# The end of a feed-forward sweep: gated residual on seven sums and one accumulation for the last two down steps, in all three sweeps

## The chip, the core and the metric

The kernel runs on one core of a Trainium2 chip. The core has five engines with their own instruction streams: TensorE (PE, matrix products), VectorE (DVE), ScalarE (ACT), GpSimd (POOL) and SyncE (SP, which here issues all transfers between the DRAM and the on-chip memory). Matrix products are written to PSUM, of which this part of the kernel uses eight banks of 512 columns. The metric is the time of one execution on the device in microseconds (us).

## The reference

One layer of a diffusion backbone on 2048 latent tokens and 128 context tokens of width 1024. A first half (two kinds of linear recurrence between an input and an output projection) gives the residual stream `x2`. The second half, which the change touches, is

```
h  = rms_norm(x, norm2) * (1 + sc2) + sh2
ff = (silu(h @ w_gate) * (h @ w_up)) @ w_down      # 1024 -> 2816 -> 1024
x  = x + g2 * ff
y  = rms_norm(x, norm_f)
```

`g2` is a row of 1024 gates, one row for all latent tokens and another for the context tokens. All is float32.

## The kernel before

The tokens are 17 tiles of 128 rows. The feed-forward part runs in three sweeps over tiles: sweep 0 has 5 (the context tile `NL` first, then four of latent tokens), sweeps 1 and 2 have 6 latent tiles each. In each sweep the hidden width is walked in 11 steps `fp` (0 to 10) of 256 columns. A step computes the gate product and the up product of its columns for all tiles of the sweep (two calls of `unit`), multiplies them (L1476) and multiplies the result by 256 rows of `w_down` (a down step), which is added to the sweep's output `acc`, one tile of 128x1024 for each tile of tokens.

Each float32 factor is split into a high and a low part (`split`: ACT rounds, DVE or POOL subtracts), and a product is three matmuls. `unit` multiplies by blocks with seven products in place of eight (`z`, L1209): 12 matmuls a product, 14 products in a step. In sweep 0 the weight parts for this are made (loads `wr`, sums on POOL, splits) and also stored to DRAM (`wpd`); sweeps 1 and 2 load them from there (`wp`, 512 KB a part, four buffers). In sweeps 1 and 2 the down steps 0 to 8 also work by seven sums (`down_seven`, y of L1367), which `combine` puts together in step 9. Step 9 and 10 of every sweep, and all steps of sweep 0, are plain (`down`, y of L1406: groups of six matmuls for one step, one tile of tokens and one half `n` of the 1024 columns), added to `acc` from PSUM by DVE (L1410).

Groups of a down step are not run at once: they are put in the list `pending`, and `unit` takes some from it after each of its products (`tick`). The groups of the last two steps (`rest`) run behind step 10.

The end of a sweep differs. In the last sweep step 10 loads the gate `g2` and puts one `residual` for each tile in `pending`: DVE multiplies `acc` by the gate (L1252), POOL adds `x2` from DRAM (L1253). The last two down steps are then one group of twelve matmuls for each tile and half; DVE multiplies it by the gate out of PSUM (L1413, tile `yg`), POOL adds it to `acc` (L1415, DVE for the last tile), and `finish` normalises the tile (squares `jk` on ACT, small instructions on DVE, a last one at L1262) and stores it. The four blocks of `w_down` of step 10 (`wds10`) are put in `wp` buffers. In sweeps 0 and 1 the last two steps are two groups of six with two adds on DVE, and residual and finish of each tile (`close`) are put in `pending` in step 0 of the next sweep.

Behind step 10 of sweeps 0 and 1 the token parts of the next sweep (`stored_parts`, loads `hr`, splits into `x1` to `x7`) and the first weight parts (`uw`) are also prepared.

Two sets of buffers are shared by much of this: `raw6`, four tiles of 128x1024 (`wr`, `wdr` for the rows of `w_down`, `hr`, `x2`, the gate, `norm_f`), and `wp`. There are three PSUM banks for `y` and five for `z`. A list scheduler sets the order of instructions on each engine when the program is built, by program order and its own estimate of times; on the chip each engine keeps that order.

Of the kernel before, what the change touches and what calls it, by code (L numbers as in the profile page):

```python
# [33 lines left out]
def hybrid_step(ctx: ExitStack, tc, x, vecs, ada1, ada2, bada, win, wgt, alog, dtb, sa, sb, wout, wg, wu, wd, normf,  # L34
# [1008 lines left out]
    with ExitStack() as s6:  # L1043
# [232 lines left out]
        def wd_part(a, tile=None):  # L1276
            t = halves_of(tile() if tile else fl.tile([P, 2, 512], F32R, tag="wd", name="wd", bufs=5))
            split(a, *t)
            return t

        def wd_blocks(fp, tile=None):

            out = {}
            rs = wd_raw(fp)
            for n in range(2):
                for j in range(2):
                    out[n, j] = wd_part(rs[j][:, 512 * n:512 * n + 512], tile)
            return out
# [98 lines left out]
        def down(ts_, steps, N, first=False, end=False):  # L1387

            n2 = len(ts_) // 2
            if end:  # L1390
                nf = load_nf()

            def group(ti, n):
# [17 lines left out]
                else:  # L1411
                    yg = fe.tile([P, 512], F32, tag="st", name="yg", bufs=2)
                    nc.vector.tensor_tensor(out=yg, in0=py, in1=g2[0][:, cs], op=ALU.mult)  # L1413
                    e = nc.vector if ti == len(ts_) - 1 else nc.gpsimd
                    e.tensor_tensor(out=acc[c][:, cs], in0=yg, in1=acc[c][:, cs], op=ALU.add)  # L1415
                if n and end:
                    finish(c, acc[c], nf)

            idx = range(len(ts_))
            return [lambda i=i, n=n: group(i, n) for i, n in  # L1420
                    ([(i, n) for i in idx for n in range(2)] if end else [(i, n) for n in range(2) for i in idx])]

# [10 lines left out]
        for sw, ts_ in enumerate(sweeps):  # L1433
# [9 lines left out]
            for fp in range(NP):  # L1443
                if fp == 0 and sw:

                    nf = load_nf()
                    g2[0] = load_g2()

                    def close(c):
                        residual(c)  # L1450
                        finish(c, acc[c], nf)

                    pending.extend([lambda c=c: close(c) for c in sweeps[sw - 1]])
                if fp == NP - 1:
                    wds9 = wd_blocks(NP - 2)
                    if last:
                        g2[0] = load_g2()
                        pending.extend([lambda c=c: residual(c) for c in ts_])
# [31 lines left out]
            wds10 = wd_blocks(NP - 1, (lambda: wp_tile().rearrange("p a k f -> p a (k f)")) if last else None)  # L1490
            if last:
                rest = down(ts_, [(last_hid, wds9), (hid, wds10)], N, end=True)
            else:
                rest = down(ts_, [(last_hid, wds9)], N) + down(ts_, [(hid, wds10)], N)
# [65 lines left out]
```

## Time and profile before

| what | value |
|---|---|
| median of 3 runs | 3359.61 us (3348.92 to 3360.17) |
| the profiled execution | 3358.57 us, span of the trace 3356.9 us |
| PE busy | 3121.5 us, 93% of the span |
| DVE, ACT, POOL busy | 2089.0, 1519.0, 1254.8 us |
| the feed-forward sweeps | some 1860 to 3357 us of the span |

Times in rows are us from the start of the span. A row of the windows view gives the stretch, its length, then for each engine the time it was busy and (x) its instructions, the granted clock of TensorE as a share of full speed, the share of time that the 16 transfer engines were busy, and GB/s. A row of the timeline gives start, length, engine, line, instruction, out<-in, shape and, in brackets, the idle time before it and what ended it. Matmuls are pipelined: the length of one reaches into the next, so the pitch is read from the starts.

### The profile page before, as it was taken

How to read it: one execution, taken by the hardware profiler on the slowest of the kernel's cores; microseconds unless marked ns; L12 is line 12 of the kernel's file. 1: busy time of each engine (PE TensorE's matmuls, PEld its weight loads, DVE VectorE, ACT ScalarE, POOL GpSimd, SP SyncE). 2: the span in 40 equal slices, each digit the busy share in tenths (PEclk: the TensorE clock that was granted, in tenths of full speed). 3: DMA queues.
4: the chain of work that ended last, by engine and by line, in shares of the span. 5: the costliest groups of instructions: out<-in, count | busy, mean ns of one | idle time of the engine just before them, and what ended most of it. 6: DMA issues, size and time to landing. Idle time of an engine off the chain costs nothing. (4 is left out here: it accounts for less than half of the span.)

```text
span 3356.9 us, 51604 instructions
## 1 busy us (share of the span) xinstructions
PE 3121.5 (93%) x18550; PEld 2792.2 (83%) x18550; DVE 2089.0 (62%) x4016; ACT 1519.0 (45%) x3233; POOL 1254.8 (37%) x1228
## 2 busy tenths in 40 slices
PE   7899989999999799998897999999999999899998
PEld 4687779999998677877786888888899998799997
DVE  4667744474553764564666777778565677565667
ACT  6455435374464544663764555454422223422222
POOL 1100001021121337413566544554545553544446
PEclk8999999999999988999998999999999999999999
DMA  5235410111114667877784877898656766655564
GB/s 221 72 109 145 116 55 29 53 44 36 53 39 138 172 179 230 265 249 253 240 263 152 304 287 286 298 325 314 223 192 212 240 211 230 228 193 194 184 201 155
DMA packets 331009, 620.12 MB, mean 185 GB/s; under 512 B 77818, under 2 KB 177954, under 8 KB 324354
## 3 DMA queue, kind: packets, MB, share of 16 engines
q1 hardware_dynamic: 330754, 616.83, 56.0%
q8 instruction: 147, 2.41, 0.3%
q14 instruction: 108, 0.88, 0.1%
HBM read 435.22 MB, written 181.51 MB: 184 GB/s over the span
## 5 line engine op out<-in xcount | busy, mean ns | idle before, releaser
L257 PE MATMUL pj<-hh,wh 128*128 128x384 f32 (+2 forms) x1480 | 546.0, 369 | 12.9 <-DVE q L464 6.6
L257 PE MATMUL pj<-hl,wh 128*128 128x384 f32 (+2 forms) x1480 | 545.2, 368 | 0.3 <-POOL hl L231 0.3
L257 PE MATMUL pj<-hh,wl 128*128 128x384 f32 (+2 forms) x1480 | 545.3, 369 | 0.0
L257 PEld LDWEIGHTS pj<-hh,wh 128*128 128x128 f32 (+1 forms) x1480 | 280.4, 189 | 45.5 <-DVE q L464 6.8
L257 PEld LDWEIGHTS pj<-hl,wh 128*128 128x128 f32 (+1 forms) x1480 | 280.1, 189 | 29.9 <-issue 3.1
L257 PEld LDWEIGHTS pj<-hh,wl 128*128 128x128 f32 (+1 forms) x1480 | 280.1, 189 | 28.7 <-issue 3.3
L1476 POOL TENSOR_TENSOR u<-u,g 128x384 f32<-128x384 f32 (+1 forms) x132 | 136.3, 1033 | 292.7 <-DVE u L1217 242.8
L494 POOL TENSOR_SCALAR th<-th,nlbh,lbh 128x384 f32<-128x384 f32 (+1 forms) x40 | 60.5, 1513 | 405.8 <-ACT G L492 401.8
L1371 DVE TENSOR_TENSOR acc<-y,acc 128x512 f32<-128x512 f32 x192 | 131.7, 688 | 64.9 <-PE y L1367 58.0
L1209 PE MATMUL z<-x1h,wp 128*128 128x384 f32 (+1 forms) x528 | 142.8, 334 | 17.6 <-ACT wp L1067 14.2
L1067 ACT ACTIVATE wd<-wdr 128x512 fp32r<-128x512 f32 x146 | 90.0, 627 | 149.4 <-PE y L1367 95.4
L1367 PE MATMUL y<-wd,hid0h 128*128 128x512 f32 x432 | 136.4, 399 | 18.7 <-ACT hid0h L1067 10.0
L1464 ACT ACTIVATE g<-g 128x384 f32<-128x384 f32 (+1 forms) x132 | 66.7, 505 | 191.0 <-DVE g L1217 190.1
L1067 ACT ACTIVATE hid0h<-u 128x384 fp32r<-128x384 f32 (+3 forms) x113 | 53.3, 481 | 217.2 <-POOL u L1476 181.2
L1209 PE MATMUL z<-x6h,wp 128*128 128x384 f32 (+1 forms) x528 | 142.7, 333 | 7.2 <-ACT wp L1067 4.6
L246 DVE TENSOR_TENSOR wl<-raw,wh 128x512 fp32r<-128x512 f32 (+1 forms) x74 | 51.7, 698 | 153.6 <-ACT wh L245 153.5
L1371 DVE TENSOR_TENSOR sum<-y,sum 128x512 f32<-128x512 f32 x144 | 99.3, 690 | 75.8 <-PE y L1367 73.3
L1209 PE MATMUL z<-x4h,wp 128*128 128x384 f32 (+1 forms) x528 | 144.5, 331 | 1.3 <-DMA wp<-wpd 1.3
L1209 PE MATMUL z<-x7h,wp 128*128 128x384 f32 (+1 forms) x528 | 144.3, 332 | 1.0 <-DMA wp<-wpd 1.0
L1068 DVE TENSOR_TENSOR wd<-wdr,wd 128x512 fp32r<-128x512 f32 x146 | 111.9, 775 | 51.5 <-ACT wd L1067 50.6
L1209 PE MATMUL z<-x3h,wp 128*128 128x384 f32 (+1 forms) x528 | 142.6, 328 | 0.0
L1209 PE MATMUL z<-x2h,wp 128*128 128x384 f32 (+1 forms) x528 | 140.5, 328 | 1.4 <-DMA wp<-wpd 1.4
(414 smaller groups left out, 8850.6 us busy)
## 6 DMA issues: line engine op xcount, KB each, us to landing
wp<-wpd SPq DMA_DIRECT2D x308, 512.0 KB
wpd<-wp SPq DMA_DIRECT2D x154, 512.0 KB
ld<-qkvd SPq DMA_DIRECT2D x34, 1024.0 KB
wdr<-in_wd_dram SPq DMA_DIRECT2D x66, 512.0 KB
raw<-in_win_dram SPq DMA_DIRECT2D x72, 256.0 KB
e<-grd SPq DMA_DIRECT2D x68, 256.0 KB
at<-in_ada_dram SPq DMA_DIRECT2D x64, 256.0 KB
wr<-in_wg_dram SPq DMA_DIRECT2D x22, 512.0 KB
```

Of the source, the lines that this page charges most:

```text
L246: nc.vector.tensor_tensor(out=wl[:, ks], in0=raw, in1=wh[:, ks], op=ALU.subtract)
L257: nc.tensor.matmul(out=out, lhsT=a[:, k], rhs=b[:, k], start=t == 0, stop=t == 3 * KD - 1)
L494: nc.gpsimd.tensor_scalar(out=th, in0=th, scalar1=nlbh[:, col:col + 1], scalar2=lbh[:, col:col + 1], op0=ALU.mult, op1=ALU.add)
L1067: nc.scalar.activation(out=wh, in_=raw, func=AF.Copy)
L1068: (e or nc.vector).tensor_tensor(out=wl, in0=raw, in1=wh, op=ALU.subtract)
L1209: nc.tensor.matmul(out=z, lhsT=w_[:, k], rhs=x_[:, k, :N], start=t == 0, stop=t == 3 * HK - 1)
L1367: nc.tensor.matmul(out=py, lhsT=u_[:, j * P:j * P + P], rhs=v_, start=t == 0, stop=t == 2)
L1371: nc.vector.tensor_tensor(out=sums[i, j], in0=py, in1=sums[i, j], op=ALU.add)
L1464: nc.scalar.activation(out=g, in_=g, func=AF.Silu)
L1476: nc.gpsimd.tensor_tensor(out=us[i], in0=us[i], in1=gs[i], op=ALU.mult)
```

## The change

In all three sweeps the gate is loaded and the residual runs in step 10 (on what the first nine steps have summed), and the last two down steps are one group of twelve matmuls whose result is multiplied by the gate and added. In sweeps 0 and 1 `finish` stays in `pending` of step 0 of the next sweep; the last sweep keeps its finish behind each tile (`lastone`). The context tile has its own gate, which `gate2` loads once in its residual and once in its down groups; its two groups run first, one behind the other. Three of the four blocks `wds10` are put in `wp` buffers in sweeps 0 and 1, the fourth in a `wd` buffer (in the last sweep all four, as before).

```diff
-        def wd_part(a, tile=None):
-            t = halves_of(tile() if tile else fl.tile([P, 2, 512], F32R, tag="wd", name="wd", bufs=5))
+        def wd_part(a, lent=False):
+            t = halves_of(wp_tile().rearrange("p a k f -> p a (k f)") if lent
+                          else fl.tile([P, 2, 512], F32R, tag="wd", name="wd", bufs=5))
...
-                    out[n, j] = wd_part(rs[j][:, 512 * n:512 * n + 512], tile)
+                    out[n, j] = wd_part(rs[j][:, 512 * n:512 * n + 512], 2 * n + j < lent)
...
-        def down(ts_, steps, N, first=False, end=False):
+        def down(ts_, steps, N, first=False, end=False, lastone=False):
...
-            if end:
+            if lastone:
                 nf = load_nf()
+            gm = {}
...
                 else:
+                    if c not in gm:
+                        gm[c] = gate2(c)
                     yg = fe.tile([P, 512], F32, tag="st", name="yg", bufs=2)
-                    nc.vector.tensor_tensor(out=yg, in0=py, in1=g2[0][:, cs], op=ALU.mult)
-                    e = nc.vector if ti == len(ts_) - 1 else nc.gpsimd
+                    nc.vector.tensor_tensor(out=yg, in0=py, in1=gm[c][:, cs], op=ALU.mult)
+                    e = nc.vector if lastone and ti == len(ts_) - 1 else nc.gpsimd
                     e.tensor_tensor(out=acc[c][:, cs], in0=yg, in1=acc[c][:, cs], op=ALU.add)
-                if n and end:
+                if n and lastone:
                     finish(c, acc[c], nf)
...
+            own = [(i, n) for i in idx for n in range(2) if lastone or end and ts_[i] == NL]
             return [lambda i=i, n=n: group(i, n) for i, n in
-                    ([(i, n) for i in idx for n in range(2)] if end else [(i, n) for n in range(2) for i in idx])]
+                    own + [(i, n) for n in range(2) for i in idx if (i, n) not in own]]
...
                     nf = load_nf()
-                    g2[0] = load_g2()
-
-                    def close(c):
-                        residual(c)
-                        finish(c, acc[c], nf)
-
-                    pending.extend([lambda c=c: close(c) for c in sweeps[sw - 1]])
+                    pending.extend([lambda c=c: finish(c, acc[c], nf) for c in sweeps[sw - 1]])
                 if fp == NP - 1:
                     wds9 = wd_blocks(NP - 2)
-                    if last:
-                        g2[0] = load_g2()
-                        pending.extend([lambda c=c: residual(c) for c in ts_])
+                    g2[0] = load_g2()
+                    pending.extend([lambda c=c: residual(c) for c in ts_])
...
-            wds10 = wd_blocks(NP - 1, (lambda: wp_tile().rearrange("p a k f -> p a (k f)")) if last else None)
-            if last:
-                rest = down(ts_, [(last_hid, wds9), (hid, wds10)], N, end=True)
-            else:
-                rest = down(ts_, [(last_hid, wds9)], N) + down(ts_, [(hid, wds10)], N)
+            wds10 = wd_blocks(NP - 1, 3 + last)
+            rest = down(ts_, [(last_hid, wds9), (hid, wds10)], N, end=True, lastone=last)
+            if not last:
                 fresh_parts()
```

## Rows read from the trace of the kernel before

**Rows 1.** Windows view, stretches of the feed-forward part.

```profile
2252.00:2266.00 14.00, 14.00 (x87) 13.21 (x86) 11.19 (x20) 6.13 (x12) 5.15 (x5) 1.00 1.00 372
2266.00:2280.00 14.00, 14.00 (x97) 14.00 (x96) 9.52 (x13) 7.08 (x16) 14.00 (x12) 1.00 0.81 298
2280.00:2293.00 13.00, 12.89 (x85) 12.36 (x84) 9.28 (x16) 5.26 (x10) 6.35 (x8) 1.00 1.01 374
2293.00:2325.00 32.00, 31.75 (x144) 26.19 (x143) 30.58 (x47) 16.22 (x30) 4.99 (x6) 1.00 0.87 309
2325.00:2376.00 51.00, 36.99 (x180) 33.32 (x179) 38.77 (x64) 22.78 (x52) 29.64 (x20) 0.90 0.83 281
2797.00:2851.00 54.00, 52.50 (x253) 45.33 (x251) 42.39 (x62) 20.29 (x40) 12.70 (x8) 1.00 0.63 206
2851.00:2895.00 44.00, 31.02 (x132) 27.45 (x132) 33.47 (x59) 22.40 (x47) 31.59 (x24) 0.85 0.77 262
2925.00:3250.00 325.00, 325.00 (x1703) 304.35 (x1702) 197.50 (x310) 81.34 (x150) 153.60 (x142) 1.00 0.59 193
3260.00:3317.00 57.00, 53.05 (x277) 49.91 (x276) 43.53 (x47) 9.40 (x18) 49.61 (x29) 0.97 0.67 227
```

**Rows 2.** Waits of PE, 2330 to 2400: us in total, times, longest.

```profile
PE y L1367 <- ACT wd L1067: 7.1, 1, 7.1
PE z L1209 <- DMA wp<-wpd: 2.5, 3, 1.4
PE y L1367 <- POOL hid0l L1068: 2.0, 1, 2.0
```

**Rows 3.** Timeline of ACT at the first seam.

```profile
2351.80 0.63 ACT L747 ACTIVATE jk<-acc 128x512 f32<-128x512 f32 x1 [1.77 <-POOL acc L1253]
...
2353.04 0.61 ACT L1067 ACTIVATE wd<-wdr 128x512 fp32r<-128x512 f32 x1
```

**Rows 4.** Waits of PE, 2845 to 2920.

```profile
PE y L1367 <- ACT hid0h L1067: 8.6, 2, 6.7
PE y L1367 <- ACT acc L1369: 2.9, 1, 2.9
```

**Rows 5.** Timeline of PE, two products behind the wait at 2353.71.

```profile
2355.15 0.52 PE L1209 MATMUL z<-x4h,wp 128*128 128x384 f32 x1
...
2358.67 0.52 PE L1209 MATMUL z<-x4h,wp 128*128 128x384 f32 x1
...
2361.61 0.34 PE L1209 MATMUL z<-x5h,wp 128*128 128x384 f32 x1
...
2363.73 0.34 PE L1209 MATMUL z<-x3h,wp 128*128 128x384 f32 x1
```

**Rows 6.** Instructions by source line: count, ns min/median/max, first and last start.

```profile
L1410 DVE TENSOR_TENSOR acc<-y,acc x124: 671/678/692, 1929.8 to 2849.8; 128x512 f32<-128x512 f32 x124
...
L1252 DVE TENSOR_TENSOR acc<-acc,g x17: 1199/1435/3396, 2320.3 to 3290.7; 128x1024 f32<-128x1024 f32 x17
...
L1253 POOL TENSOR_TENSOR acc<-acc,x x17: 2337/2392/3354, 2327.5 to 3302.9; 128x1024 f32<-128x1024 f32 x17
...
L1415 POOL TENSOR_TENSOR acc<-yg,acc x10: 1283/1292/1312, 3319.3 to 3343.1; 128x512 f32<-128x512 f32 x10
```

**Rows 7.** Waits of PE at the end of the last sweep, 3285 to 3357.

```profile
PE z L1209 <- DVE g L1217: 2.4, 1, 2.4
```

**Rows 8.** Timeline of POOL at the end of sweep 0.

```profile
2262.91 1.29 POOL L1071 TENSOR_TENSOR s<-wr 128x512 f32<-128x512 f32 x1 [3.94 <-DMA wr<-in_wg_dram]
...
2298.22 1.47 POOL L1068 TENSOR_TENSOR hid0l<-u,hid0h 128x256 fp32r<-128x256 f32 x2
```

**Rows 9.** Timeline of PE, last product of sweep 0 and first groups behind it.

```profile
2292.80 0.31 PE L1209 MATMUL z<-x3h,wp 128*128 128x320 f32 x1
2292.94 0.63 PE L1406 MATMUL y<-wd,hid0h 128*128 128x512 f32 x2
...
2294.33 0.62 PE L1406 MATMUL y<-wd,hid0h 128*128 128x512 f32 x2
```

More of the change, by code (lines that the diff above doesn't have):

```diff
@@ L1274, in wd_raw, with wd_blocks @@
             return rs
-        def wd_part(a, tile=None):
-            t = halves_of(tile() if tile else fl.tile([P, 2, 512], F32R, tag="wd", name="wd", bufs=5))
+        def wd_part(a, lent=False):
+            t = halves_of(wp_tile().rearrange("p a k f -> p a (k f)") if lent
+                          else fl.tile([P, 2, 512], F32R, tag="wd", name="wd", bufs=5))
             split(a, *t)
             return t
-        def wd_blocks(fp, tile=None):
+        def wd_blocks(fp, lent=0):
             out = {}
```

## The prediction, made before the changed kernel ran

> **What bounds the kernel now.** I read the page first, for the engines' shares, then cut the feed-forward part into stretches by the windows view, then asked the waits of TensorE (PE) in the stretches where it was not full, and last the timeline of single engines there. The page's shares say that PE bounds the whole, so a change to the other engines is worth only the PE time that it frees or takes. The windows [rows 1] show where there is any: in the steady part of the third sweep PE is busy 325.00 of 325 us, but at the seam of sweeps 0 and 1 (2325 to 2376) it is busy 36.99 of 51 us, so 14.0 us idle, and at the seam of sweeps 1 and 2 (2851 to 2895) 31.02 of 44 us, so 13.0 us. The down steps just ahead of that second seam (2797 to 2851) lose another 1.5 us. These 28.5 us are all that the edit can free directly.
>
> What ends the idle time there? At the first seam one wait of 7.1 us for ScalarE's (ACT) split of a `wd` tile, 2.0 us for a POOL split of `hid0l`, and 2.5 us for `wp` loads [rows 2]. The long one is a queue: on ACT the square of the norm (`jk`) stood ahead of the `wd` split and itself waited 1.77 us for POOL's residual add; the split came right behind it [rows 3]. At the second seam ACT again is what PE waits for, 8.6 us for `hid0h` and 2.9 us for the first `acc` of the new sweep, whose buffer the old sweep's finish still held [rows 4]. So residual and finish of the old sweep, run in step 0 of the next, are what stalls PE at both seams.
>
> PE also pays in clock. Behind the 7.1 us wait a product of 12 matmuls takes 2355.15 to 2359.19 = 4.04 us; the next product's 12 run from 2361.61 to the start of the one behind it at 2363.73, 2.12 us [rows 5]. That is the lower of the clock's two levels, and costs 1.9 us per seam stall. At the second seam two waits (6.7 and 2.9 us) come before such a product and the mean granted clock is 0.85 [rows 1, 4]; I take 3 us there.
>
> Recoverable in all: 14.0 + 1.9 + 13.0 + 3 + 1.5 = 33.4 us.
>
> **The change, part by part.** *Matmuls.* The same products in the same number, 12 in a group in place of twice 6. Worth 0 for PE.
>
> *Evacuation.* The 124 adds of L1410 [rows 6] include 2 x 5 x 2 = 20 of the last two steps of sweep 0 and 24 of sweep 1; they become 10 and 12 multiplications by the gate of the same size on VectorE (DVE), and as many adds on POOL at 1.29 us [rows 6]. At their 0.68 us sweep 0 saves 10 x 0.68 = 6.8 us of DVE in a stretch where DVE is busy 30.58 of 32 us (2293 to 2325), and POOL, busy 4.99 us there, takes on 12.9 [rows 1]. PE idles only 0.25 us there, so this gives next to nothing itself; it is room.
>
> *The residual* leaves step 0 of the next sweep: 5 and 6 gate multiplications (1.2 to 3.4 us each on DVE) and POOL adds of 2.39 us [rows 6], with their `x2_d` loads on SP. Only `finish` stays. At the seam this takes 12 and 14 us of POOL work and 7 to 9 us of DVE work away, and lets the first `wd` rows be loaded without waiting behind the residual's tiles in `raw6`. The finish itself can start tile by tile during the last down groups, and PE has the next 14 products (some 30 us at 2.12 us each) before it needs the first `wd`. So I let the ACT and POOL waits go. What is late next is the `wp` load: `wds10` now sits in three of four `wp` tiles until its groups are done, so where four weight parts of the next sweep lay ready at the seam, one does. A product lasts 2.12 us, which gives a following load about three products' time. The waits on these loads were 2.5 and about 1 us; I leave 4 us at each seam (bounds 1 and 8). Gain at the seams: 33.4 - 8 = 25.4 us.
>
> *Where the residual goes:* step 10 of sweeps 0 and 1. The last sweep already has it there and is the model for sweep 1: from 3260 to 3317 PE is busy 53.05 of 57 us [rows 1], 3.95 us idle, of which 2.4 us is a wait for a DVE evacuation of `z` standing behind residual work [rows 7]. Sweep 1 pays 4 us (bounds 1 and 7).
>
> For sweep 0 the trace has no model, and it is the crowded one: it also splits and stores the weights. In step 10 the DMA share is 1.00, 0.81 and 1.01 in three stretches from 2252 to 2293, and POOL is busy 14.00 of 14 us in the middle one [rows 1]. Into it go five residual loads and two gate loads (the context tile loads its own gate twice, in the residual and in its down groups), 7 x 0.52 MB = 3.7 MB, 9.9 us at the 372 GB/s of the first stretch; 5 POOL adds, 12 us; and the gate tile keeps one of four `raw6` slots to the sweep's end. Queued behind the loads on SP are the weights of step 10, and POOL already stands 3.94 us for such a load [rows 8]. From below the cost is 0: the holes of the 0.81 stretch (2.7 us) and later loads of `hr` absorb the bytes, and the adds run from 2300 on, where POOL is free, as late as the first new add into `acc`. From above 9.9 + 12 = 22 us, everything exposed. I take 8, nearer to the lower end, because what must be on time for PE is weights alone, and these need POOL for only part of their seven parts.
>
> *The new chain needs step 10's `hid` and `wds10` at its seventh matmul.* Before, 10 groups of 1.4 us (2292.94 to 2294.33 for the first [rows 9]) of step 9 stood ahead. In sweep 0 the last product starts its last matmul at 2292.80 and the last `hid` split ends at 2298.22 + 1.47 = 2299.69 [rows 8, 9], 6.9 us. The groups of the first half of the tokens come first, three of 2.8 us in sweep 1 and at least three in sweep 0, and need only the early two of the four `us`, so 8.4 us cover 6.9. Cost 0; without that cover 5 us per sweep. `wds10` in lent `wp` tiles is within the 8 us and 4 us taken.
>
> **Sum.** -25.4 + 4 + 8 = -13.4 us on the profiled execution's 3358.57 us: 3345.2. The median of the runs is 1.0 us above that execution, so 3346.
>
> A rule speaks against the edit: the Trainium skill (SBUF — State Buffer, Who interferes with whom) has a DVE instruction with two SBUF inputs contend with a GpSimd one that reads SBUF. The `x` splits of the next sweep are such instructions; the gate multiplication out of PSUM is not. The trace agrees as far as L1252, two SBUF inputs, ranges from 1199 to 3396 ns [rows 6]; rival D is what it would make.
>
> **The rivals.** *A, all of sweep 0's cost is hidden* and each seam keeps 2 us: -33.4 + 4 + 4 = -25, 3335 us. For it: POOL is nearly idle from 2300 to 2325 and the DMA has holes. Against it: shares of 1.00.
>
> *B, the weights starve (slower).* Place: `raw6` in step 10 of sweep 0. Two weight pairs are wanted there together; the gate tile leaves three slots, and residual tiles, earlier in the program, take the third and then those of the first pair. Each of the step's two units then waits for a pair that is loaded only when the pair before is freed: 2 x 0.52 MB at 372 GB/s 2.8 us, two POOL sums 2.6 us, a split 1.3 us, in all 6.7 us, twice, with 12 us of residual adds ahead of the sums on POOL: 25 us; with the 4 of sweep 1 that is 29 against 25.4, so 3363. It decides from 21 us on in sweep 0; with late `hid` and low clock behind every stall it reaches 41 us there, 45 in all, and 3379. For it: POOL waits for just these loads already [rows 8]. Against: PE is full in the two stretches up to 2280 [rows 1] with that load as late as it is.
>
> *C, the stall is replaced.* `finish` with its ACT chain stays in the same step and holds `acc` and ACT as before, half of each seam's loss stays (17 us): -17 + 12 = -5, 3355 us. For it: the square `jk` now waits for a POOL add that comes only behind the last down group. Against it: 30 us of products lie between.
>
> *D, DVE bounds the last groups of sweep 0.* If every POOL add held up a split for its whole length, DVE's 30.6 us become 30.6 - 6.8 + 12.9 = 36.7 us where PE needs some 32: 4.7 us more at the first seam, -8.7, 3351 us. Against: in the stretch with POOL at 14.00 of 14, DVE still did 9.52 us of work [rows 1].
>
> **How the numbers follow.** Half a per cent, 16.8 us, is about what a measurement of this kernel tells from no change. Chances: the forecast 0.38 (3336 to 3354), A 0.24, B 0.18, C 0.12, D 0.08. Faster by over 0.5% means below 3342.8: nearly all of A and a third of the forecast, 0.35. Slower by over 0.5% is above 3376.4: two thirds of B, 0.12. Same: 0.53. The range reaches from below A (3328, the whole 33.4 us less 2) to the middle of B's reach (3370), leaving out some 0.07 below and 0.12 above.
>
> **What would show it.** Right: at both seams PE's idle time falls from 14.0 and 13.0 us to 4 or less, with the ACT waits for `wd` and `hid0h` gone from its list; `wp` loads head it. Sweep 1's step 10 shows a wait of 2 to 3 us for DVE on `z`; sweep 0's step 10 shows waits for `wp` splits of 8 us in sum. Wrong: stalls of over 10 us in step 10 of sweep 0 (B), or ACT waits that stay at the seams (C), or evacuations that hold PE between 2293 and 2325 (D).

## The result and the profile after

The changed kernel takes 3385.86 us (median of 4 runs, 3380.64 to 3390.26), the kernel before 3355.07 us beside it; the ratio is 1.0092, 95% interval [1.0066, 1.0118]. It is slower by 0.9%, outside the range of the prediction. The profiled execution has a span of 3388.4 us, against 3356.9. PE's busy time is 6.0 us longer, 3127.5 us against 3121.5; the other 25.5 us of the loss are idle time.

To place it I cut every trace at the last matmul of each sweep's last product (`z<-x3h`, as 2292.80 in [rows 9]). Sweep 0, from its first product to there, went from 444.4 to 465.9 us (+21.5); the second stretch, to the same point of sweep 1, from 502.3 to 520.4 (+18.1); the third from 521.0 to 510.2 (-10.8). With 2.5 us of a later first product and 0.3 us in the tail that is 31.6 us, for the 31.5 between the spans.

These cuts lie at the same product, not at the same amount of PE's work. Counted in the traces, the changed kernel has run 12 more matmuls of down steps ahead of the first cut (558 against 546) and 16 more ahead of the second (1248 against 1232), because the first halves of its long groups start early. At some 0.23 us each (six from 2292.94 to 2294.33 in [rows 9]) 2.8 us of sweep 0's 21.5 are work done early, 0.9 us of the second stretch's 18.1, and the third stretch owes 3.7 of its 10.8 us to the same.

The windows view after, to be read against [rows 1] (PE is the first pair behind the length, the clock the third number from the right):

```profile
2252.00:2317.00 65.00, 50.05 (x299) 46.70 (x298) 39.11 (x57) 20.18 (x41) 35.42 (x28) 0.89 0.81 281
2317.00:2342.00 25.00, 10.28 (x32) 6.95 (x30) 18.15 (x27) 15.82 (x30) 6.20 (x7) 0.66 0.87 301
2342.00:2400.00 58.00, 52.18 (x239) 46.58 (x240) 31.36 (x67) 22.88 (x46) 25.98 (x20) 0.91 0.66 220
...
2830.00:2880.00 50.00, 43.69 (x195) 37.03 (x194) 36.98 (x49) 21.92 (x42) 24.92 (x18) 0.93 0.56 194
2880.00:2930.00 50.00, 44.96 (x241) 42.11 (x240) 28.02 (x69) 27.66 (x57) 27.00 (x22) 1.00 0.86 295
```

Step 10 of sweep 0, where PE had been all but full, now idles 15.0 us; the first seam idles 14.7 + 5.8 = 20.5 us where it had idled 14.0; at the second seam 5.0 us are left of 13.0, but 6.3 us are new just ahead of it (2830 to 2880). In step 10 and in the first part of the seam (2252 to 2342) the DMA share is 0.81 to 0.87 and POOL and DVE have idle time: no engine is full there.

The waits of PE after, first 2250 to 2400, then 2770 to 2960, stand against [rows 2, 4]:

```profile
PE z L1209 <- ACT wp L1067: 13.3, 2, 12.7
...
PE z L1209 <- ACT x1h L1067: 11.1, 1, 11.1
PE z L1209 <- DMA wp<-wpd: 3.4, 2, 3.2
PE y L1368 <- ACT hid0h L1067: 2.4, 1, 2.4
PE y L1409 <- DVE yg L1418: 1.8, 1, 1.8
...
PE z L1209 <- DVE u L1217: 2.2, 1, 2.2
PE z L1209 <- DMA wp<-wpd: 1.7, 3, 1.1
...
PE y L1409 <- DVE yg L1418: 6.3, 1, 6.3
PE y L1368 <- ACT hid0h L1067: 2.3, 1, 2.3
```

The 7.1 us for `wd` and the 8.6 us for `hid0h` are gone from the seams, as meant. Four waits of the new ending itself have come: 12.7, 11.1, 1.8 and 6.3 us. The first names ACT, but ACT only waits too; SP's timeline shows for what:

```profile
2257.59 0.32 SPq L1242 DMA_DIRECT2D g<-modd  x1
...
2269.27 0.36 SPq L1251 DMA_DIRECT2D x<-x2d  x1
...
2282.89 0.41 SPq L1242 DMA_DIRECT2D g<-modd  x1
...
2286.99 8.15 SPq L1251 DMA_DIRECT2D x<-x2d  x4
2297.12 0.33 SPq L1093 DMA_DIRECT2D wr<-in_wu_dram  x1
2299.42 0.33 SPq L1094 DMA_DIRECT2D wr<-in_wu_dram  x1
...
2337.20 0.32 SPq L1242 DMA_DIRECT2D g<-modd  x1
```

The second weights of step 10 (`wr` of `wu`) are loaded 19.7 us ahead of the sweep's last matmul (2316.78). In the trace before they were loaded 32.6 us ahead of it:

```profile
2260.22 0.88 SPq L1093 DMA_DIRECT2D wr<-in_wu_dram  x1
2261.19 0.44 SPq L1094 DMA_DIRECT2D wr<-in_wu_dram  x1
```

Ahead of them in the program stand the residual's tiles, all in `raw6`: the latent gate, five `x2` rows, and the context tile's own gate, which is issued only at 2282.89. SP keeps its order as the engines do, and its waits from 2255 to 2305 show two reasons for the delay. The stores of weight parts (L1103) between the loads wait for DVE's splits, and loads wait for tiles that POOL's adds still use (L1251 `x2`, L1093 and L1094 the weights):

```profile
SPq L1103 <- DVE wp L1068: 27.3, 12, 7.5
SPq L1251 <- POOL acc L1253: 4.4, 2, 2.4
SPq L1093 <- POOL acc L1253: 1.9, 1, 1.9
SPq L1094 <- POOL acc L1253: 1.9, 1, 1.9
```

PE's first matmul with the late weights is the first of these rows:

```profile
2302.14 0.64 PE L1209 MATMUL z<-x1h,wp 128*128 128x320 f32 x1 [12.72 <-ACT wp L1067]
...
2335.90 0.69 PE L1209 MATMUL z<-x1h,wp 128*128 128x384 f32 x1 [11.08 <-ACT x1h L1067]
...
2341.98 0.74 PE L1409 MATMUL y<-wd,hid0h 128*128 128x512 f32 x2 [1.79 <-DVE yg L1418]
```

The second row is the next sweep's first product, which waits for ACT's split of a late `hr` row. It stands on PE's queue behind the third of the ten long groups and ahead of the other seven, for the first three (two of them the context tile's) keep all three `y` banks until the context gate, loaded at 2337.20 behind the `hr` rows, lets DVE evacuate them:

```profile
2341.24 1.29 DVE L1418 TENSOR_TENSOR yg<-y,g 128x512 f32<-128x512 f32 x2 [1.17 <-DMA g<-modd]
```

### The profile page after: what moved, and what is told of

It reads as the page before. It is cut to its first block, busy times and chain, and to the rows that moved or that the text cites. A ratio compares the mean times of both kernels' runs of the same rounds, so it can differ in the third digit from the quotient of the medians.

```text
span 3388.4 us, 51627 instructions
## 1 busy us (share of the span) xinstructions
PE 3127.5 (92%) x18550; PEld 2795.2 (82%) x18550; DVE 2068.0 (61%) x3994; ACT 1521.1 (45%) x3235; POOL 1288.9 (38%) x1250
## 4 chain that ended last, share of the span: by engine, by line
PE 38%; DMA 7%; POOL 5%; DVE 5%; ACT 4%; issue 3%; SPq 1%; POOLq 0%; DVEq 0%; ACTq 0%
PE z L1209 18%; PE y L1368 8%; PE py L847 3%; PE y L1409 3%; DMA wdr<-in_wd_dram 1%; PE pS L938 1%; POOL u L1475 1%; DMA wp<-wpd 1%; PE po L947 1%; ACT L126 1%; PE pa L954 1%; ACT jk L747 1%; DVE wp L1068 1%; POOL acc L1253 1%; PE pj L257 1%
## 5 line engine op out<-in xcount | busy, mean ns | idle before, releaser
L494 POOL TENSOR_SCALAR th<-th,nlbh,lbh 128x384 f32<-128x384 f32 (+1 forms) x40 | 60.6, 1515 | 405.3 <-ACT G L492 401.4
L1209 PE MATMUL z<-x6h,wp 128*128 128x384 f32 (+1 forms) x528 | 143.5, 335 | 13.4 <-ACT wp L1067 5.5
L1217 DVE TENSOR_TENSOR u<-z,u 128x384 f32<-128x384 f32 (+1 forms) x165 | 84.9, 531 | 92.3 <-PE z L1209 91.3
L1209 PE MATMUL z<-x5h,wp 128*128 128x384 f32 (+1 forms) x528 | 139.9, 328 | 0.3 <-DMA wp<-wpd 0.3
```

Of the source, the lines that this page charges most:

```text
L494: nc.gpsimd.tensor_scalar(out=th, in0=th, scalar1=nlbh[:, col:col + 1], scalar2=lbh[:, col:col + 1], op0=ALU.mult, op1=ALU.add)
L1209: nc.tensor.matmul(out=z, lhsT=w_[:, k], rhs=x_[:, k, :N], start=t == 0, stop=t == 3 * HK - 1)
L1217: nc.vector.tensor_tensor(out=out, in0=z, in1=b, op=ALU.add)
```

## The experiments

The theories at the start: **S**, the four slots of `raw6`; **T**, throughput (bytes, POOL's and DVE's work of the residual in step 10); **Q**, the order of the program and of the queues; **L**, the long groups of twelve. Stretches are from one profiled execution each. Sweep 0 in the old form reads 443.6 to 448.2 us in six traces, so less than 5 us of difference there says nothing by itself. Most of that scatter lies in its first nine steps, which read 382.6 to 388.0 us over all runs. The last two, where the residual's work went, can be read closer: the column "steps 9, 10" runs from the first matmul of step 9's first product to the last one of the sweep's last product, 336 matmuls of products in each run, with the number of down-step matmuls between them in brackets. The old form reads 60.6 to 62.4 us there. Of each edit the telling lines are shown; `...` stands for lines left out.

| run | ratio, 95% interval | sweep 0 | steps 9, 10 | second | third |
|---|---|---|---|---|---|
| before | 1 | 444.4 | 61.0 (48) | 502.3 | 521.0 |
| after | 1.0092 [1.0066, 1.0118] | 465.9 | 81.2 (60) | 520.4 | 510.2 |
| e1 sweep 0 as before | 1.0008 [0.9995, 1.0021] | 446.3 | 60.8 (48) | 510.0 | 509.3 |
| e4 joined groups alone | 0.9998 [0.9982, 1.0013] | 445.7 | 60.6 (48) | 505.5 | 514.6 |
| e3 weights first | 1.0098 [1.0081, 1.0115] | 449.9 | 67.3 (60) | 535.3 | 510.6 |
| e2 gates apart | 1.0076 [1.0058, 1.0093] | 461.2 | 75.0 (60) | 515.1 | 516.2 |
| e6 no x2 add | 1.0098 [1.0082, 1.0114] | 464.6 | 77.4 (60) | 522.0 | 509.8 |
| e7 context gate kept | 1.0062 [1.0050, 1.0075] | 466.5 | 80.6 (60) | 508.3 | 510.1 |
| e5 gates and x2 aside | 1.0054 [1.0041, 1.0067] | 458.0 | 73.5 (60) | 511.9 | 514.8 |
| e11 e5 without x2 | 1.0041 [1.0026, 1.0055] | 451.9 | 67.4 (55) | 509.3 | 514.9 |
| e13 e5 without residual | 1.0030 [1.0016, 1.0043] | 449.6 | 62.9 (56) | 511.3 | 515.3 |
| e9 e2 and blocks apart | 1.0053 [1.0038, 1.0069] | 462.4 | 74.4 (60) | 515.7 | 513.1 |
| e12 e11 and blocks aside | 1.0023 [1.0008, 1.0038] | 450.8 | 65.6 (56) | 507.0 | 515.6 |
| e8 e1, sweep 1 aside | 1.0009 [0.9993, 1.0025] | 448.2 | 62.3 (48) | 506.2 | 512.1 |
| e10 e8 and blocks aside | 1.0009 [0.9998, 1.0020] | 448.0 | 62.4 (56) | 506.6 | 510.6 |
| e14 x2 left at the finish | 1.0018 [1.0004, 1.0033] | 453.9 | 68.2 (56) | 512.5 | 508.0 |
| e15 the same, sweep 1 alone | 0.9986 [0.9975, 0.9997] | 443.6 | 60.8 (48) | 509.2 | 504.1 |

**e1, sweep 0 ends in the old way, sweep 1 in the new.**

```diff
-                    g2[0] = load_g2()
-                    pending.extend([lambda c=c: residual(c) for c in ts_])
+                    if sw:
+                        g2[0] = load_g2()
+                        pending.extend([lambda c=c: residual(c) for c in ts_])
...
```

> Sweep 0 ends as in the kernel before (residual and finish in step 0 of sweep 1, two groups of six), sweep 1 ends in the new way. Clock of the sweeps, from the trace: first product of sweep 0 to its last 444.4 us before and 465.9 us changed, last of sweep 0 to last of sweep 1 502.3 and 520.4, last of sweep 1 to last of sweep 2 521.0 and 510.2. Theory S (slots: the gate and the residual's tiles in raw6 make the weights and token parts of sweep 0 late): the loss belongs to sweep 0, so 444, 506 (4 more for the residual in step 10 of sweep 1) and 510: some 7 us faster than before, ratio 0.998. Rival T (throughput: bytes, POOL and DVE work of the residual are too much in step 10 of sweep 0): the same here. Rival L (the long groups themselves cost, in any sweep): the third stretch stays at 516 or more, no faster than before.

3355.46 us against 3352.5. The whole loss is gone with sweep 0's part. Sweep 1's part gains 11.7 us in the third stretch and gives back 7.7 in the second; 3.7 us of both are 16 matmuls that run ahead of the cut between them. PE waits 2.2 us for `u` ahead of that cut and 5.8 us for `yg` behind it (to 2815.53, the cut is at 2805.90).

**e4, the kernel before with the two last down steps joined, and three blocks in `wp`; the residual stays where it was.**

```diff
...
-                rest = down(ts_, [(last_hid, wds9)], N) + down(ts_, [(hid, wds10)], N)
+                rest = down(ts_, [(last_hid, wds9), (hid, wds10)], N)
```

> The kernel before, with the last two down steps of sweeps 0 and 1 in one group of twelve and one DVE add, and three of the last blocks in wp tiles; no gate, residual and finish stay in step 0 of the next sweep. S, T, Q: within 5 us of before (3350 to 3360), seams as before. L: slower by 6 to 15 us, from waits of the long groups for the last blocks and for DVE ahead of the seam.

3350.84 us: no change that can be told. L falls. The waits for `wp` loads at the seams are 5.2 and 4.8 us in sum, so the lent blocks are felt, but they take the place of others.

**e3, sweep 0's residual put into `pending` behind the second weights.**

```diff
-                    pending.extend([lambda c=c: residual(c) for c in ts_])
+                    if sw:
+                        pending.extend([lambda c=c: residual(c) for c in ts_])
...
                 uw = weight_parts(1, fp, sw)
+                if fp == NP - 1 and not sw:
+                    pending.extend([lambda c=c: residual(c) for c in ts_])
```

> The changed kernel, with the residuals of sweep 0 put in the list only behind the loads of the second weights of step 10 (program order alone; slots, bytes and work as in the changed kernel). Theory Q (queue: the residual's loads stand ahead of the weights in program order, slots would do): the wait of 12.7 us goes, first stretch below 453, second no longer than 520, total 3365 to 3375. S: what the weights win the residual and the token parts lose, since the same tiles share the same slots: first stretch 453 to 458, second 525 to 532, total 3378 to 3390. T: as S.

3383.44 us. The 12.7 us wait is gone and comes back one user later, on the rows of `w_down`:

```profile
PE y L1409 <- ACT wp L1067: 17.6, 1, 17.6
...
PE z L1209 <- ACT x1h L1067: 11.7, 1, 11.7
```

Q as the cause falls: another order moves the wait and removes none of it. S and T both allow this.

**e2, the gates in idle tiles of the seven sums.**

```diff
-            gm = raw_tile("g2")
-            dma(out=gm, in_=mod_d[c2:c2 + 1, 3 * D:4 * D].broadcast_to([P, D]))
+            for n in range(2):
+                t = f"sum{(1, 5)[c2]}{n}"
+                gm.append(fl.tile([P, 512], F32, tag=t, name=t))
+                dma(out=gm[n], in_=mod_d[c2:c2 + 1, 3 * D + 512 * n:3 * D + 512 * n + 512].broadcast_to([P, 512]))
```

> The changed kernel, with the gates in tiles of the seven sums (idle in sweep 0, free after they are put together in sweeps 1 and 2) in place of two raw6 tiles; same bytes, same work, the residual's multiplication in two halves. S: the wait of 12.7 us for the second weights of step 10 falls below 6, the context gate comes early and the 11.1 and 1.8 us waits behind it fall below 5 together; first stretch 452 to 458 in place of 465.9, second 505 to 512 in place of 520.4; 3352 to 3366 us in all. T: all waits stay within 3 us, 3380 to 3390. L: no change in the third stretch.

3376.36 us, by the ratios some 5 us less than the changed kernel, with intervals that overlap. The waits of 12.7, 11.1 and 1.8 us are gone; in their place stand 4.8 us for DVE and 3.0 us for ACT on `wp`, 8.9 and 7.6 us for `wp` loads at the seams and 6.9 us for `u` in sweep 1. The slots taken by the gates are a part of the loss only.

**e6, POOL's add of `x2` in sweep 0 left out.**

```diff
-            nc.gpsimd.tensor_tensor(out=y, in0=y, in1=x2, op=ALU.add)
+            if c not in sweeps[0]:
+                nc.gpsimd.tensor_tensor(out=y, in0=y, in1=x2, op=ALU.add)
```

> The changed kernel with POOL's add of x2 in the residual of sweep 0 left out (five adds of 2.4 us; the x2 rows are still loaded into raw6, the gate multiplication stays): a tile is free as soon as its row has landed. Theory S, with the slots held because POOL's adds come late: the 12.7 us wait falls to 4 us or less and the ratio comes down from 1.009 to 1.003 to 1.006 (the context gate's 11.1 us stay). Theory T with the bytes as the bound: the wait stays above 9 us, ratio 1.007 or more. Together with the run that moves the tiles: if both take the wait away it is slots held by POOL; if only this one does it is POOL's work itself.

3388.53 us, ratio 1.0098: nothing gained, though POOL does 12 us less. Waits of 9.0 us for `wp` and 14.3 us for `x1h` stay. Steps 9 and 10 are 3.8 us shorter, but the wait for `x1h` is 3.2 us longer. So S in the form "slots held by POOL's adds" is refuted as the main cause, and so is T with POOL as the engine. The result is as T with the bytes foretold it; the tiles still pass through `raw6` ahead of the weights, though, so bytes and slots aren't told apart here. The next run but one does that.

**e7, the context tile's gate loaded once and kept.**

```diff
-            return load_g2(1)
+            if not cg:
+                for n in range(2):
+                    cg.append(fl.tile([P, 512], F32, tag=f"sum5{n}", name=f"cg{n}"))
+                    dma(out=cg[n], in_=mod_d[1:2, 3 * D + 512 * n:3 * D + 512 * n + 512].broadcast_to([P, 512]))
+            return cg
```

> The changed kernel with the context tile's gate loaded once, in the residual, and kept in two idle sum tiles until the context tile's groups; all else stays. If the late second load of that gate behind the hr rows is a cause of its own: the 11.1 us wait on x1h and the 1.8 us on yg at the first seam fall to 3 us or less in sum, and the time falls by 8 to 13 us, ratio 1.005 to 1.007. If it is only a shadow of the late weights (everything behind the 12.7 us wait is late anyway): less than 4 us of gain, ratio 1.008 or more, and waits for x1h or wp stay at that place.

3376.14 us. The second stretch falls by 12.1 us, with the waits for `x1h` and `yg` at the first seam, and sweep 0 is as in the changed kernel (466.5). So the late gate is a cause of its own, about 10 us by the ratios and 12 by the stretch. The interval lies apart from that of e6, measured beside it, though not from the wide one of the changed kernel itself. On PE's queue the groups now run on where the next sweep's product had stood.

**e5, gates and `x2` rows of sweeps 0 and 1 in idle sum tiles.**

```diff
+                    t = "sum" + ("12", "52", "60", "61", "62")[aside[1] % 5]
+                    aside[1] += 1
+                    x2 = fl.tile([P, 512], F32, tag=t, name="x26s")
+                    dma(out=x2, in_=x2_d[c][:, h])
+                    nc.vector.tensor_tensor(out=y[:, h], in0=y[:, h], in1=gm[n], op=ALU.mult)
+                    nc.gpsimd.tensor_tensor(out=y[:, h], in0=y[:, h], in1=x2, op=ALU.add)
```

> The changed kernel with the gates and the x2 rows of the residual of sweeps 0 and 1 in the nine idle tiles of the seven sums (as halves of 512), so that raw6 is left to the weights, the rows of w_down and hr. Bytes, POOL's and DVE's work stay as they are. Theory S (the loss is the four slots of raw6, which residual tiles hold in program order ahead of the second weights): the 12.7 us wait for wp in step 10 of sweep 0 falls to 3 us or less, sweep 0 loses 5 us or less against before in place of 21, the late context gate goes too, and the ratio to before comes to 0.993 to 1.000. Theory T (the loss is throughput: 3.7 MB more and 12 us more of POOL's work in a stretch that is full of both): sweep 0 still loses 12 us or more, in waits for wp spread over ACT, DVE and DMA, and the ratio stays above 1.004.

3369.96 us. Both theories missed: S by the total, T by the long wait, which is gone. With the same bytes and work, the weights of `wu` are loaded 33.3 us ahead of the sweep's last matmul again (at 2306.22), and no wait in step 10 is over 2 us:

```profile
2272.89 0.33 SPq L1093 DMA_DIRECT2D wr<-in_wu_dram  x1
```

But sweep 0 is still 13.6 us longer than before. Steps 9 and 10 hold 12.5 of them: 5.8 us of idle time in short waits, 2.8 us of matmuls that run early, and a granted clock of 0.95 where it had been 1.00. And the first seam has a new wait on the stored weights of sweep 1:

```profile
PE z L1209 <- DMA wp<-wpd: 12.3, 3, 9.8
```

**e11, e5 without the `x2` loads and adds of sweep 0; e13, without its gate multiplications too.**

```diff
-                    x2 = fl.tile([P, 512], F32, tag=t, name="x26s")
-                    dma(out=x2, in_=x2_d[c][:, h])
...
-                    nc.gpsimd.tensor_tensor(out=y[:, h], in0=y[:, h], in1=x2, op=ALU.add)
+                    if c not in sweeps[0]:
+                        x2 = fl.tile([P, 512], F32, tag=t, name="x26s")
+                        dma(out=x2, in_=x2_d[c][:, h])
+                        nc.gpsimd.tensor_tensor(out=y[:, h], in0=y[:, h], in1=x2, op=ALU.add)
```

e13 is e11 with this besides:

```diff
-                    nc.vector.tensor_tensor(out=y[:, h], in0=y[:, h], in1=gm[n], op=ALU.mult)
+                    if c not in sweeps[0]:
+                        nc.vector.tensor_tensor(out=y[:, h], in0=y[:, h], in1=gm[n], op=ALU.mult)
```

> The run with gates and x2 rows of sweeps 0 and 1 aside (3370 us, ratio 1.0054, sweep 0 13.6 us longer than before), with the x2 loads and POOL's adds of sweep 0's residual left out (2.6 MB and 12 us of POOL less; the gates and their multiplications stay). Theory T for the rest of sweep 0's loss (bytes and POOL's work): sweep 0 comes down to 3 us or less over before, ratio 1.0015 to 1.003. Rival (the gate multiplications on DVE in front of the z evacuations and splits, or the gates' loads): sweep 0 stays 9 us or more over, ratio 1.004 or more.

> The run with gates and x2 aside, with the whole residual of sweep 0 left out (no gate multiplication, x2 load or add; the gates are loaded, the groups multiply by them). Where only x2 was left out, sweep 0 was 451.9 us, 7.5 us over before. Theory DVE (the gate multiplications stand in front of z evacuations and wp splits): sweep 0 comes to 444 to 447 us and the ratio from 1.004 to 1.002. Rival (order of the instructions on the engines, the long groups or the gates' loads): sweep 0 stays at 450 us or more, ratio 1.003 or more.

3370.53 and 3364.19 us. Sweep 0 falls from 458.0 to 451.9 and 449.6, the ratio from 1.0054 to 1.0041 and 1.0030. Neighbouring intervals overlap (the median of e11 is no lower than that of e5), so in the times only the sum of both steps is near to being shown. Steps 9 and 10 tell the runs apart. Their windows before, after, in e5, e11 and e13, in this order:

```profile
2231.80:2292.80 61.00, 60.89 (x384) 58.25 (x385) 46.18 (x71) 27.74 (x53) 36.88 (x31) 1.00 0.91 340
...
2235.55:2316.78 81.23, 66.28 (x396) 61.90 (x396) 52.22 (x75) 27.35 (x52) 45.28 (x34) 0.92 0.82 290
...
2232.67:2306.22 73.55, 67.75 (x396) 62.89 (x397) 59.91 (x81) 28.62 (x55) 52.85 (x40) 0.95 0.86 304
...
2230.56:2297.97 67.41, 63.71 (x391) 59.59 (x391) 57.09 (x83) 29.61 (x57) 36.81 (x30) 1.00 0.89 323
...
2233.70:2296.55 62.85, 62.73 (x392) 59.77 (x392) 47.40 (x71) 29.06 (x56) 35.54 (x30) 1.00 0.92 337
```

With 0.23 us taken off for each matmul more than before (12, 12, 7 and 8), the four lose 17.4, 9.8, 4.8 and 0.0 us. So of the loss in these steps some 8 us go with the tiles out of `raw6`, some 5 with the loads and adds of `x2`, some 5 with DVE's gate multiplications, and nothing is left in e13, where PE idles 0.1 us. The rest of e13's longer sweep 0 lies in its first nine steps, within their scatter.

**e9, e2 with blocks of step 10 in idle sum tiles in place of `wp`; e12, the same on e11; e10, the same in sweep 1 alone (on e8, below).**

```diff
+            if lent and blk_at:
+                t = tuple(fl.tile([P, 512], F32R, tag="sum" + blk_at.pop(0), name="wds") for _ in range(2))
+                split(a, *t)
+                return t
...
+            blk_at[:] = ["12", "52", "60", "61"] if sw == 0 else ["12", "52", "60", "61", "50", "51"]
```

> The run with the gates apart (3376 us, ratio 1.0076; waits for wp loads of 8.9 us at the first seam, 7.6 us at the second), and the blocks of w_down of step 10 put in idle sum tiles in place of wp: two of the three lent in sweep 0, all three in sweep 1. Theory W (wds10 in the wp tiles keeps the next sweep's stored weights from being loaded): the waits for wp loads at the seams fall to 3 us or less each, the time falls by 8 to 13 us to a ratio of 1.004 to 1.005. Rival Q2 (the loads are late in SP's order, behind hr and x2): the waits stay above 5 us, ratio above 1.0065.

> The run with gates and x2 aside and sweep 0's x2 left out (3370.5 us, ratio 1.0041; one wait for wp loads of 9.6 us at the first seam), with two of the three lent blocks of step 10 of sweep 0 in sum tiles. Theory W (the lent wp tiles are what the wait at the first seam is): it falls to 2 us or less and the time by 6 to 10 us, ratio 1.001 to 1.0025. Rival H (the stall is handed on to the next work in the queue, as it was in sweep 1, where two waits of 5.4 us went and the time stayed): the wait falls, others of 4 us or more appear at that seam, ratio 1.003 or more.

3375.02 us (ratio 1.0053, from 1.0076) and 3362.76 us (1.0023, from 1.0041). In e9 the `wp` waits fall from 8.9 to 1.2 us and from 7.6 to 3.0 us, so theory W, that lent blocks keep the stored weights out, is right about the waits; 5.1 us for `yg` and 5.4 us for DVE's `acc` (L1268) stand at the first seam instead. In e12 the longest falls from 9.6 to 3.6 us. Both intervals overlap those of the runs that they start from.

**e8, e1 with sweep 1's gate and `x2` in idle sum tiles** (the edit of e5, for sweep 1 alone)**, and e10, that with two of the lent blocks aside** (the edit of e9; first line e8, the rest e10).

```diff
+            aside[0] = sw == 1
...
-                    t = "sum" + ("12", "52", "60", "61", "62")[aside[1] % 5]
+                    t = "sum" + ("12", "52", "62")[aside[1] % 3]
...
+            blk_at[:] = ["50", "51", "60", "61"] if sw == 1 else []
```

> Sweep 0 ends as in the kernel before, sweep 1 in the new way (3355.5 us and a ratio of 1.001 when it stood alone), with sweep 1's gate and x2 rows in the idle sum tiles. Theory S: the waits of step 10 of sweep 1 (5.8 us for yg, 2.2 us for u, some us for wp) are slots too, hr comes some 30 us earlier, the second stretch costs 3 us or less in place of 7.7, the third keeps its gain of 11 to 12: ratio 0.996 to 0.998. Theory T: they are DVE's and POOL's work, the waits stay, ratio 1.000 to 1.002.

> The run with sweep 0 as before and sweep 1's gate and x2 rows aside (3359 us, ratio 1.0009; waits for wp loads of 5.4 us at the next sweep's first product and 5.4 us at its fourth), with two of the three lent blocks of step 10 in sum tiles, x2 on three sum tiles. Theory W: both waits fall to 2 us or less, the time falls by 7 to 10 us, ratio 0.997 to 0.999. Rival Q2: they stay above 4 us each, ratio 1.000 to 1.002.

Ratio 1.0009 both times. e8 turns the 5.8 us for `yg` into 0.8, and 12.1 us of waits for `wp` loads come; e10 cuts these, and shorter waits on others come. From the waits of PE, 2780 to 2900, first e8:

```profile
PE z L1209 <- DMA wp<-wpd: 12.1, 4, 5.4
PE y L1431 <- DVE yg L1440: 0.8, 1, 0.8
```

and e10:

```profile
PE z L1209 <- DMA wp<-wpd: 7.2, 7, 1.9
PE z L1209 <- DVE x1l L1068: 2.4, 1, 2.4
PE z L1209 <- ACT x1h L1067: 2.1, 1, 2.1
```

Each edit did to its wait what it should, and the time did not follow.

**e14, only the gate multiplication in step 10 of sweeps 0 and 1; `x2` is loaded and added ahead of the finish in the next step 0, as before. Gates and blocks as in e9. e15, the same for sweep 1, with sweep 0 as before.**

```diff
+        def close(c, nf):
+            x2 = raw_tile("x26")
+            dma(out=x2, in_=x2_d[c])
+            nc.gpsimd.tensor_tensor(out=acc[c], in0=acc[c], in1=x2, op=ALU.add)
+            finish(c, acc[c], nf)
...
-                    pending.extend([lambda c=c: finish(c, acc[c], nf) for c in sweeps[sw - 1]])
+                    pending.extend([lambda c=c: close(c, nf) for c in sweeps[sw - 1]])
```

In e15 the finish of sweep 0 is that of the kernel before:

```diff
                         if sw == 1:
                             residual(c)
+                        else:
+                            add_x2(c)
                         finish(c, acc[c], nf)
```

> The run with gates and blocks apart (3375 us, ratio 1.0053), with only the gate multiplication in step 10 of sweeps 0 and 1; the x2 rows are loaded and added ahead of the finish in the next sweep's step 0, as before. If x2's loads and POOL's adds in step 10 are most of what is left: sweep 0 falls to 452 us or less, sweep 1's step 10 loses 3 us or less, and the ratio comes to 0.998 to 1.002. If the seams gained just because the x2 adds had left them: the ACT waits for wd and hid0h come back there at 5 us or more each, and the ratio stays at 1.003 or more.

> Sweep 0 ends as in the kernel before; in sweep 1 only the gate multiplication is in step 10, x2 is loaded and added ahead of the finish in the next sweep's step 0, the gate and the blocks of step 10 are in idle sum tiles. If x2's loads and POOL's adds in step 10 take the gain of sweep 1 back: sweep 0 446 to 448 us, the second stretch 503 to 507, the third 508 to 511, together 4 to 10 us less than before, ratio 0.997 to 0.999. If it is the longer chain of the joined groups, or the order of the instructions: the second stretch is 507 us or more and the ratio 1.000 to 1.002.

e14 takes 3362.28 us: 1.0018 in place of e9's 1.0053, their intervals apart. The ACT waits at the seams return at 3.9 and 3.7 us, not at the 5 that I had set against it. e15 takes 3346.09 us against 3350.5: ratio 0.9986 [0.9975, 0.9997], the only form whose interval lies below 1, by 4 us. It ends close to 1, and this is one of fifteen forms, so the gain is weakly shown. The second stretch is longer than the 503 to 507 us expected and the third shorter than its 508 to 511; but 18 more matmuls (4.2 us) run ahead of the cut between them, and without these the two are 505.0 and 508.3, as the better theory has them, and so is the ratio. The second seam in the windows view of e15 (2853 to 2897, shifted by 2 us against [rows 1], as the end of sweep 1 is):

```profile
2853.00:2897.00 44.00, 40.50 (x203) 36.88 (x202) 24.30 (x41) 21.24 (x40) 26.28 (x22) 0.96 0.77 257
```

PE idles 3.5 us there in place of 13.0, at a granted clock of 0.96 in place of 0.85.

## Why the prediction was wrong

**The step that failed first** is the 8 us for step 10 of sweep 0, taken "nearer to the lower end, because what must be on time for PE is weights alone, and these need POOL for only part of their seven parts". The stretch grew by 21.5 us: of these some 2.8 us are matmuls that run early, 1.2 us lie in the first nine steps, within their scatter, and 17.4 us are lost in steps 9 and 10. I had priced the added work by engine: 9.9 us of bytes, 12 us of POOL. Where slots don't bind, the work alone costs 9.8 us (e5), not far from the 8; some 5 of them are DVE's gate multiplications, which that sum left out. What it had at nothing is room: `raw6` hands its four tiles out in program order, the residual's seven came ahead of the second weights, and a tile can't be loaded until an older one is done with. That is the other 7.7 us. Moving the tiles out of `raw6` took the long wait away with bytes and work unchanged (e5), and putting them behind the weights only moved it (e3).

This was rival B, given 0.18, and its place and mechanism came as told, with two exceptions. Of its two waits only the second unit's stands in PE's list, once with 12.7 us in place of twice 6.7. And POOL's adds were 12 us of its price, where leaving them out gained 3.8 us in these steps and nothing in the whole (e6). The time lies above even B's 3379.

**The step that was left out** is the context tile's second gate load. I counted it among 3.7 MB and saw neither that it is issued behind the next sweep's `hr` loads nor that the groups which need it run first and keep all three `y` banks. It costs about 10 us (e7). With it the second stretch, forecast at 14.0 + 1.9 - 4 - 4 = 7.9 us less, came out 18.1 us more; with the gate kept it is still 6.0 us more. So the gain of the first seam failed beyond the gate: between 2308 and 2400 of e7 PE waits 10.7 us in sum (4.1 for `wp` loads, 3.4 for `hid0h`, the rest for DVE and others), where 14.0 us were idle before and 4 us were forecast.

**The second seam's gain was real.** The third stretch was forecast at -13 - 3 - 1.5 + 4 = -13.5 us and measured -10.8, -11.7 in e1. In both 3.7 us are work done ahead of the cut, and the wait for `yg` (6.3 and 5.8 us), which is part of the price of the new ending, stands in this stretch. Without both it is -13.4 and -13.8. The ACT waits went, as told. The `wp` loads are 3.4 us at the first seam of the changed kernel, within the 4 that I had left (bounds 1 and 8), but behind longer stalls; in e5, where those are relieved, they are 12.3 us, above the bound. Rival C, a stall that `finish` keeps up, did not happen: 2.4 and 2.3 us for `hid0h`.

**Sweep 1's step 10** was forecast at 4 us from the last sweep's model. The waits for `u` and `wp` are 3.9 us, as the model has them. The 6.3 us for `yg` are not in it, because the last sweep has no next sweep whose `x` splits stand ahead of `yg` on DVE. Here they do, from 2838.34 on, with gaps of 0.6 us at most; the last of them and the first `yg` behind them:

```profile
2844.57 0.68 DVE L1068 TENSOR_TENSOR x1l<-hr,x1h 128x512 fp32r<-128x512 f32 x1
2845.17 1.48 DVE L1068 TENSOR_TENSOR x2l<-hr,x2h 128x512 fp32r<-128x512 f32 x1
2846.57 0.68 DVE L1418 TENSOR_TENSOR yg<-y,g 128x512 f32<-128x512 f32 x1
```

The rate of exchange is then nearly even: e1 comes out at 1.0008.

**"Cost 0" for the late `hid` and for joining the groups** was right: e4 is at 0.9998, and no wait for `hid1` is over 1 us in the changed kernel.

**Rival D**, DVE slowed by POOL, did not decide. The effect is there, in DVE's timeline of the changed kernel:

```profile
2289.44 1.48 DVE L1217 TENSOR_TENSOR g<-z,g 128x320 f32<-128x320 f32 x3
2302.12 1.29 DVE L1068 TENSOR_TENSOR wp<-wr,wp 128x512 fp32r<-128x512 f32 x2 [11.21 <-ACT wp L1067]
...
2309.88 0.48 DVE L1217 TENSOR_TENSOR u<-z,p 128x320 f32<-128x320 f32 x1
...
2310.88 1.36 DVE L1068 TENSOR_TENSOR wp<-s,wp 128x512 fp32r<-128x512 f32 x1
```

The split at 2310.88, with POOL at work for the first 0.8 us, takes 1.36 us; the two at 2302.12, with POOL waiting, 1.29 us together. The additions out of PSUM take 0.49 us each at 2289.44, beside a POOL add, and 0.48 us at 2309.88 without one. The Trainium skill (SBUF — State Buffer, Who interferes with whom) says that a DVE instruction with two SBUF inputs contends with a GpSimd one that reads SBUF, and that one with at most one SBUF input, outside certain fast modes, does not; the trace agrees, by those numbers.

**What stays open.** The 7.7, 5 and 5 us of sweep 0 are read from one execution each, and every build has its own order on the engines; in e5 the order of SP's loads and stores changed with the slots, so the two aren't told apart. How the 5 us with `x2` divide between bytes and POOL isn't settled. What keeps the first seam at 10.7 us of waits in e7 wasn't tested. Why freeing `wp` in e10 gave nothing is seen in the waits that replace it, not tested one by one.

## What to carry to other kernels

Before moving work into a stretch, list the tiles that it takes from every shared set of buffers, in program order, and ask which load comes next in that order; engine shares and bytes don't show this bound. Price the moved work on every engine that does a part of it. A load that is issued late for the group that runs first costs the whole queue behind it, so load it early (running that group last wasn't tried). Of a step to be moved, move the part that takes no buffer from the crowded set: here the multiplication could go in sweep 1 (e15), and the rows had better stay (e14 against e9). And where a trace is cut at a landmark, count the work on both sides before two stretches are compared.

## What the runs showed of the hardware

A wait is named after the engine that came last, and that engine can itself have been starved: through the 12.7 us wait "for ACT" DVE sits idle 11.21 us for the same split, with DMA at 0.81 of its time over the stretch and the missing load issued at 2297.12. And the low clock adds to each such wait: 2317 to 2342 has a granted clock of 0.66, and behind the 11.08 us wait eleven steps of a product take 3.95 us (2335.90 to 2339.85), where a whole product of twelve takes 2.12 us at full clock [rows 5].
